# Two of four weight sums made by adding DMAs, and two groups of seven products in every gate-and-up block of FFN 2

## The chip, the cores and the metric

The kernel runs on one core of a Trainium2 chip. The metric is device time in microseconds (us), as the median of several runs. The engines are named as in the profile: PE (TensorE, matmuls), PEld (its weight loads), DVE (VectorE), ACT (ScalarE), POOL (GpSimd) and SP (SyncE, which issues most DMAs). L512 is line 512 of the kernel.

## What is computed

One layer of an encoder for 256 rows of width 2048, in float32. The parts that matter here are its two feed-forward halves:

```
x += 0.5 * (silu(h @ w_gate) * (h @ w_up)) @ w_down      h = RMSNorm(x)
```

with `w_gate` and `w_up` of 2048 x 5632 and `w_down` of 5632 x 2048. FFN 1 comes first, FFN 2 after the mixing part (an SSM and a stick-breaking attention, joined by `w_out`); a gated embedding ends the layer.

## The kernel before, in words

All weights are read once, in raw tiles of 512 x 512 (1 MB, `raw`, five buffers). To keep float32 precision, each half of a raw tile (128 x 1024) is split into two float32r parts: ACT casts it (`whi`, L181) and DVE subtracts the cast from it (`wlo`, L184). The activations are split likewise. A product is then three matmuls in place of one: high x high, low x high and high x low (L305, L306, L310 in `gemm_half`; L480, L481, L483 in `Seven.product`).

FFN gate and up run over blocks f = 0 to 10 of 512 columns. In a block, gate and up each need four quarters of the inner dimension (512 rows each, kb = 0 to 3), for two row tiles. There are two ways to do a quarter:

- `column` (L524): one side's quarter, two halves of a raw tile, 24 matmuls of 128x512 and 2 splits; gate and up together 48 matmuls and 4 splits.
- `chunk` (L490): gate and up of the quarter together in seven products (Strassen's scheme in Winograd's form), each 6 matmuls, 42 in all. The activation's four sums are made once (`sum_forms`). The weights' four sums are made for each group by DVE (`add`, L485 to L488): t1 = b11 + b12, t2 = t1 + b22, t4 = t2 + b21, t3 = b12 + b22, where b11 and b21 are the halves of gate's raw tile, b12 and b22 those of up's. Each of the seven operands is split; the sums' parts are called `shi` and `slo` (three buffers each), those of plain weights `whi` and `wlo` (four each). The sums lie in a tag `sum` of two buffers.

A block thus takes 186 matmuls with one group and 180 with two. FFN 2's blocks 1 to 10 alternate: odd blocks have two groups (`two`, L590), even blocks one. FFN 1 has plain blocks to f = 6, one group in 7 and 9 and two in 8 and 10. The down projections use groups as well, three in each FFN, by a written plan (L673 to L676).

The banks of the seven products are read when their last group is done: `opened` (L575) and `gated` (L580) by copies and adds of ACT and DVE, then L606 and L608, and two block transposes (L216).

The recorded program is put in order by a scheduler: each engine's instructions stand in one fixed order, and an engine that waits for one holds all behind it. `step()` lets helpers put their small work between the products. POOL issues few DMAs: x is written to a scratch tensor (L1453) and fetched again for each FFN's down projection (L150).

Of the kernel before, what the change touches and what calls it, by code (L numbers as in the profile page):

```python
# [13 lines left out]
ALU = mybir.AluOpType  # L14
# [19 lines left out]
def layer_kernel(ctx: ExitStack, tc: tile.TileContext, a: dict, shapes: dict, out: bass.AP):  # L34
    nc = tc.nc
# [27 lines left out]
    def uid(s):  # L63
        count[0] += 1
        return f"{s}_{count[0]}"
# [4 lines left out]
    def com(tag):  # L70
        return get(comp, tag, *{"sg": (1024, 1), "h": (1024, 2), "sq": (NB, 1), "mid": (2048, 1)}[tag])

    def phase(name):
        return tc.tile_pool(name=name, bufs=1, reuse_waits="tile")
# [24 lines left out]
    def step():  # L99
        for g in list(beside):  # L100
            if next(g, beside) is beside:
                beside.remove(g)

    def finish(g):
        for _ in g:
            pass
# [315 lines left out]
    def whole_rows(pool, parts):  # L422

        hi, lo = parts
        u = pool.tile([P, 2, NB], F32, tag="sum", name=uid("whole"), bufs=2)
        nc.vector.tensor_tensor(
            out=u.rearrange("p j n -> p (j n)"), in0=hi.bitcast(F32).rearrange("p j t -> p (j t)"),
            in1=lo.bitcast(F32).rearrange("p j t -> p (j t)"), op=ALU.add,
        )
        return u.rearrange("p j n -> p (j n)").rearrange("p (j x b) -> p j x b", j=4, b=32)  # L430

    def sum_forms(pool, u, kind="n"):

        sums = pool.tile([P, 2, NB], F32, tag="sum", name=uid("rows"), bufs=2)
        s = sums.rearrange("p j n -> p (j n)").rearrange("p (z j x b) -> p z j x b", z=4, j=2, b=32)
        (a11, a21), (a12, a22) = ([u[:, k : k + 2, 4 * t : 4 * t + 4] for t in range(TT)] for k in (0, 2))
        for z, (x, y, op) in enumerate((
            (a21, a22, ALU.subtract), (s[:, 0], a11, ALU.subtract),
            (a11, a21, ALU.subtract), (a12, s[:, 1], ALU.add),
        )):  # L440
            nc.vector.tensor_tensor(out=s[:, z], in0=x, in1=y, op=op)
        both = halves(kind)
        split(*both, sums.rearrange("p j n -> p (j n)").rearrange("p (z t) -> p z t", z=4))
        return both

    class Seven:
# [43 lines left out]
        def chunk(self, kb, final=()):  # L490

            raws = []
            for w, n0 in self.ws:
                raw = wp.tile([P, 4, NB], F32, tag="raw", name=uid("raw"), bufs=5)
                nc.sync.dma_start(
                    raw, w[4 * kb * P : 4 * (kb + 1) * P, n0 : n0 + NB].rearrange("(j p) n -> p j n", p=P)
                )
                raws.append(raw)
            b11, b21, b12, b22 = (raw[:, 2 * h : 2 * h + 2, :] for raw in raws for h in range(2))
            parts, sums = self.act(kb), self.sums(kb)  # L500

            def whole(k, t):
                return [[u[:, 2 * k + j, t * P : (t + 1) * P] for j in range(2)] for u in parts]

            def summed(z):
                return [[u[:, z, j * P : (j + 1) * P] for j in range(2)] for u in sums]

            self.product(1, whole(0, 0), b11, False, final)
            t1 = self.add(b11, b12)
            self.product(5, summed(0), t1, True, final)  # L510
            step()
            t2 = self.add(t1, b22)  # L512
            self.product(6, summed(1), t2, True, final)
            t4 = self.add(t2, b21)
            self.product(4, whole(1, 1), t4, True, final)
            step()
            t3 = self.add(b12, b22)
            self.product(7, summed(2), t3, True, final)
            self.product(2, whole(1, 0), b21, False, final)
            step()  # L520
            self.product(3, summed(3), b22, False, final)
            step()

        def column(self, side, kbs, final=False):  # L524
# [14 lines left out]
    def ffn(i, xn, nxt, bg=None):  # L539
# [23 lines left out]
        for f in range(NF):  # L563
            if prep and f == early:
                finish(prep)
                side.close()
                prep = None
                sevens = pools.enter_context(phase(f"sums{i}"))
                hp = pools.enter_context(phase(f"h{i}b"))
                sums = [sum_forms(sevens, whole_rows(sevens, xn(kb)), "h") for kb in range(2)]  # L570
            if sevens and f:
                sg, hh = com("sg"), com("h")
                gate_cols, up_cols = ([u[:, t * NB : (t + 1) * NB] for t in range(TT)] for u in (sg, hh))

                def opened(s, g=gate_cols, u=up_cols):  # L575
                    nc.scalar.copy(g[0], s.bank(1))
                    nc.vector.tensor_tensor(out=u[0], in0=s.bank(6), in1=g[0], op=ALU.add)
                    nc.vector.tensor_tensor(out=u[1], in0=s.bank(7), in1=u[0], op=ALU.add)

                def gated(s, g=gate_cols, u=up_cols, hh=hh):  # L580
                    for z, (ps, other) in enumerate(((s.bank(2), g[0]), (s.bank(4), u[1]))):
                        nc.vector.tensor_tensor(out=g[z], in0=ps, in1=other, op=ALU.add)
                        nc.scalar.activation(g[z], g[z], AF.Silu, scale=xn.rs(z))
                    v = hh.rearrange("p (t n) -> p t n", t=TT)
                    nc.vector.tensor_tensor(
                        out=v, in0=s.bank(5).unsqueeze(1).to_broadcast([P, TT, NB]), in1=v, op=ALU.subtract
                    )

                s = Seven(xn, lambda kb: sums[kb], ((wg, f * NB), (wu, f * NB)), sevens)
                two = f % 2 == (0 if bg else 1)  # L590
                if f == early:
                    s.column(0, (1, 2, 3))
                    s.chunk(0, (*shared, 2, 4))
                    put_off(0, opened, s)
                elif two:
                    s.chunk(0)
                    s.column(0, (2, 3))
                    s.chunk(1, (*shared, 2, 4))
                    put_off(0, opened, s)
                else:  # L600
                    s.chunk(0, shared)
                    put_off(0, opened, s)
                    s.column(0, (1, 2, 3), True)
                put_off(0, gated, s)
                s.column(1, (2, 3) if two and f != early else (1, 2, 3), True)
                nc.vector.tensor_tensor(out=hh, in0=s.banks[3.8], in1=hh, op=ALU.add)  # L606
                for t in range(TT):
                    nc.vector.scalar_tensor_tensor(  # L608
                        out=up_cols[t], in0=up_cols[t], scalar=xn.rs(t), in1=gate_cols[t], op0=ALU.mult, op1=ALU.mult
                    )  # L610
                put_off(2, turned, hp, f, hh)
                continue

            def gate():
                for t in range(TT):
                    nc.scalar.activation(sg[:, t * NB : (t + 1) * NB], pg[t], AF.Silu, scale=xn.rs(t))

            first = ()
            if f == 0 and bg:
                warm_up(10)  # L620
                first = first_quarters(wg, xn)
            if f == 0 and not bg:
                both = gemm_pair(xn, ((wg, 0), (wu, 0)), KD)
                pg = next(both)
                sums = [sum_forms(sevens, whole_rows(sevens, xn(kb))) for kb in range(2)]
            else:
                pg = gemm_block(xn, wg, f * NB, KD, first)
            sg = com("sg")
            if f == 0 and bg:
                for n in range(ND):  # L630
                    put_off(n, load_x, n)
                    put_off(n + 2, xn.squares, n)
                put_off(6, gate)
            else:
                gate()
            pu = gemm_block(xn, wu, f * NB, KD) if f or bg else next(both)
            if prep and f == 0:
                start(prep)
            hh = com("h")
            for t in range(TT):  # L640
                nc.vector.scalar_tensor_tensor(
                    out=hh[:, t * NB : (t + 1) * NB], in0=pu[t], scalar=xn.rs(t),
                    in1=sg[:, t * NB : (t + 1) * NB], op0=ALU.mult, op1=ALU.mult,
                )
            put_off(2, turned, hp, f, hh)
# [31 lines left out]
        for n in range(0, ND, 2):  # L677
# [17 lines left out]
            for u in plan:  # L695
                kb, final = int(u[1:]), u == plan[-1]
# [759 lines left out]
    mix.close()  # L1456

    ffn(2, n2, npl)


# [201 lines left out]
```

## Time and profile before

| what | value |
|---|---|
| median of 3 runs | 1852.45 us (1851.65 to 1853.28) |
| the profiled execution | 1852.7 us |
| its span | 1850.6 us, clock granted in full |
| ACT busy | 1027.4 us, 56% |
| POOL busy | 63.3 us, 3% |
| read from HBM | 373.46 MB, 208 GB/s with what is written over the span |

The engines work side by side, so their busy times do not add up. An idle engine costs time only where the engine that bounds the kernel waits for it. In the rows of groups, the number behind the second bar is the idle time of the engine just before these instructions, and behind the arrow is what ended it. In the rows of windows each engine has its busy time and its count of instructions; the last two columns are the mean busy share of the 16 DMA engines and the rate.

### The profile page before, as it was taken

What the parts mean: (1) busy time and instruction counts of PE and PEld (TensorE: products, weight loads), DVE (VectorE), ACT (ScalarE), POOL (GpSimd) and SP (SyncE); (2) the same over time, 40 slices, a digit from 0 to 9 for tenths busy, and PEclk for the clock granted to TensorE, in tenths of its full rate; (3) what the DMA queues carried; (4) which work ended last, traced back from release to release, by engine and by line L of the source; (5) the groups of instructions that cost most, each with busy time, mean ns of one, the idle gap of its engine ahead of it and who ended that gap; (6) DMA issues with size and microseconds to landing.
All of it is one profiled execution on the core that took longest, in us unless ns stands there. A gap on an engine that the chain in (4) does not pass through costs nothing.

```text
span 1850.6 us, 23946 instructions
## 1 busy us (share of the span) xinstructions
PE 1838.3 (99%) x9032; PEld 1518.5 (82%) x9032; DVE 1460.6 (79%) x1718; ACT 1027.4 (56%) x1187; POOL 63.3 (3%) x108
## 2 busy tenths in 40 slices
PE   9999999999999999999999999999999999999998
PEld 7888888778888888888897888888888888888887
DVE  8967665998888876687567798989898978887665
ACT  7444443655564656365685565655555555565654
POOL 0011000000000000010021000000000000000000
PEclk9999999999999999999999999999999999999999
DMA  9888868566756567675646776665656675666663
GB/s 334 281 274 277 252 217 246 173 228 200 241 196 213 192 217 248 190 262 166 216 142 218 224 262 216 235 206 198 218 198 219 207 244 185 223 195 217 208 219 125
DMA packets 232307, 406.36 MB, mean 220 GB/s; under 512 B 26784, under 2 KB 50720, under 8 KB 231904
## 3 DMA queue, kind: packets, MB, share of 16 engines
q1 hardware_dynamic: 227824, 392.81, 63.8%
q0 software_dynamic: 3648, 10.62, 1.8%
q8 instruction: 70, 1.15, 0.2%
q10 hardware_dynamic: 720, 1.41, 0.2%
q14 instruction: 45, 0.37, 0.1%
HBM read 373.46 MB, written 11.93 MB: 208 GB/s over the span
## 4 chain that ended last, share of the span: by engine, by line
PE 92%; DVE 3%; DMA 2%; ACT 2%; SPq 1%; issue 1%; DVEq 0%; ACTq 0%
PE acc L305 18%; PE acc L310 18%; PE acc L306 18%; PE aux L305 7%; PE aux L306 7%; PE aux L310 7%; PE acc L480 3%; PE acc L481 2%; PE acc L483 2%; PE aux L480 2%; PE aux L483 2%; PE aux L481 2%; DVE wlo L184 1%; SPq L1170 1%; DMA raw<-in_w_in 1%
## 5 line engine op out<-in xcount | busy, mean ns | idle before, releaser
L181 ACT CAST whi<-raw 128x1024 fp32r<-128x1024 f32 x639 | 668.1, 1052 | 684.8 <-PE acc L306 388.9
L184 DVE TENSOR_TENSOR wlo<-raw,whi 128x1024 fp32r<-128x1024 f32 x639 | 772.0, 1221 | 297.9 <-ACT whi L181 295.1
L305 PE MATMUL acc<-whi,nhi 128*128 128x512 f32 x1232 | 482.9, 392 | 1.8 <-ACT whi L181 1.7
L306 PE MATMUL acc<-whi,nlo 128*128 128x512 f32 x1232 | 479.9, 390 | 0.0
L310 PE MATMUL acc<-wlo,nhi 128*128 128x512 f32 x1232 | 340.6, 389 | 0.2 <-DVE wlo L184 0.2
L305 PEld LDWEIGHTS acc<-whi,nhi 128*128 128x128 f32 x1232 | 231.5, 188 | 52.2 <-ACT whi L181 3.0
L310 PEld LDWEIGHTS acc<-wlo,nhi 128*128 128x128 f32 x1232 | 231.2, 188 | 48.8 <-DVE wlo L184 0.6
L306 PEld LDWEIGHTS acc<-whi,nlo 128*128 128x128 f32 x1232 | 231.6, 188 | 47.2
L306 PE MATMUL acc<-whi,hlo 128*128 128x512 f32 x376 | 146.4, 389 | 0.0
L305 PE MATMUL acc<-whi,hhi 128*128 128x512 f32 x376 | 146.3, 389 | 0.0
L181 ACT CAST shi<-sum 128x1024 fp32r<-128x1024 f32 x108 | 113.4, 1052 | 43.1 <-DVE sum L487 39.6
L306 PE MATMUL aux<-whi,hlo 128*128 128x512 f32 x344 | 133.8, 389 | 0.0
L305 PE MATMUL aux<-whi,hhi 128*128 128x512 f32 x344 | 133.8, 389 | 0.0
L184 DVE TENSOR_TENSOR slo<-sum,shi 128x1024 fp32r<-128x1024 f32 x108 | 130.9, 1216 | 0.6 <-ACT shi L181 0.5
L310 PE MATMUL acc<-wlo,hhi 128*128 128x512 f32 x376 | 114.6, 389 | 0.2 <-DVE wlo L184 0.2
L310 PE MATMUL aux<-wlo,hhi 128*128 128x512 f32 x344 | 106.0, 389 | 0.0
L306 PE MATMUL aux<-whi,nlo 128*128 128x512 f32 x240 | 93.4, 389 | 0.0
L305 PE MATMUL aux<-whi,nhi 128*128 128x512 f32 x240 | 93.4, 389 | 0.0
L306 PEld LDWEIGHTS acc<-whi,hlo 128*128 128x128 f32 x376 | 70.6, 188 | 15.1 <-DVE hlo L184 0.4
L310 PEld LDWEIGHTS acc<-wlo,hhi 128*128 128x128 f32 x376 | 70.5, 188 | 15.2 <-DVE wlo L184 0.6
L305 PEld LDWEIGHTS acc<-whi,hhi 128*128 128x128 f32 x376 | 70.6, 188 | 14.6
L306 PEld LDWEIGHTS aux<-whi,hlo 128*128 128x128 f32 x344 | 64.6, 188 | 13.5
(345 smaller groups left out, 2162.6 us busy)
## 6 DMA issues: line engine op xcount, KB each, us to landing
raw<-in_ffn_w_up SPq DMA_DIRECT2D x88, 1024.0 KB, 5.8
raw<-in_ffn_w_down SPq DMA_DIRECT2D x88, 1024.0 KB, 5.1
raw<-in_ffn_w_gate SPq DMA_DIRECT2D x86, 1024.0 KB, 6.2
raw<-in_w_in SPq DMA_DIRECT2D x32, 1024.0 KB, 5.7
raw<-in_w_out SPq DMA_DIRECT2D x16, 1024.0 KB, 5.3
raw<-in_w_ple_gate SPq DMA_DIRECT2D x16, 1024.0 KB, 5.1
hT<-mid SPq DMA_DIRECT2D x160, 64.0 KB, 3.5
h<-mid SPq DMA_DIRECT2D x176, 32.0 KB, 3.6
```

Of the source, the lines that this page charges most:

```text
L181: copy = nc.scalar.copy(hi, src)
L184: nc.vector.tensor_tensor(out=lo, in0=src, in1=hi.bitcast(F32), op=ALU.subtract)
L305: nc.tensor.matmul(ps[t], lhsT=lh, rhs=hi[:, j, cols], start=start and j == 0, stop=False)
L306: nc.tensor.matmul(ps[t], lhsT=ll, rhs=hi[:, j, cols], start=False, stop=False)
L310: nc.tensor.matmul(ps[t], lhsT=lh, rhs=lo[:, j, cols], start=False, stop=stop and j == 1)
L480: nc.tensor.matmul(ps, lhsT=lh[j], rhs=hi[:, j], start=begin and j == 0, stop=False)
L481: nc.tensor.matmul(ps, lhsT=ll[j], rhs=hi[:, j], start=False, stop=False)
L483: nc.tensor.matmul(ps, lhsT=lh[j], rhs=lo[:, j], start=False, stop=z in final and j == 1)
L1170: nc.sync.dma_start(zt[0][p1 : p1 + HC, z], sv[p0 : p0 + HC, r % 2 * 2 + r // 2])
```

## The change

In `chunk`, t3 and t4 are no longer DVE's. Two DMAs issued by POOL add in place: b22 is added onto b12 in the raw tile, after t1 has read b12, and b21 is added onto t2, after product 6 has been split from it. Products 7 and 4 take their operands from there. The order of the products as written becomes 6, 5, 1, 2, 3, 7, 4. All groups are changed, in both FFNs and in the downs (27 groups before). Beside that, every block of FFN 2 from 1 to 10 has two groups (32 groups in all).

```
-            self.product(1, whole(0, 0), b11, False, final)
             t1 = self.add(b11, b12)
+            nc.gpsimd.dma_start(b12, b22, accum_op=ALU.add)
+            t2 = self.add(t1, b22)
+            self.product(6, summed(1), t2, True, final)
+            nc.gpsimd.dma_start(t2, b21, accum_op=ALU.add)
             self.product(5, summed(0), t1, True, final)
             step()
-            t2 = self.add(t1, b22)
-            self.product(6, summed(1), t2, True, final)
-            t4 = self.add(t2, b21)
-            self.product(4, whole(1, 1), t4, True, final)
-            step()
-            t3 = self.add(b12, b22)
-            self.product(7, summed(2), t3, True, final)
+            self.product(1, whole(0, 0), b11, False, final)
             self.product(2, whole(1, 0), b21, False, final)
             step()
             self.product(3, summed(3), b22, False, final)
+            self.product(7, summed(2), b12, True, final)
+            step()
+            self.product(4, whole(1, 1), t2, True, final)
             step()
...
-                two = f % 2 == (0 if bg else 1)
+                two = f % 2 == 0 if bg else True
```

In the changed kernel the adding DMAs are lines 509 and 512. Both versions of `chunk` are equally long, so all lines outside it keep their numbers.

## The prediction

> **What bounds the kernel now.** I read the page's first lines and its engine and DMA rows, then the windows of the stage that the change rebuilds, then the waits there, the chain of waits, and the DMA issues.
>
> ```profile
> span 1850.6 us, 23946 instructions
> PE 1838.3 (99%) x9032; PEld 1518.5 (82%) x9032; DVE 1460.6 (79%) x1718; ACT 1027.4 (56%) x1187; POOL 63.3 (3%) x108
> ...
> q1 hardware_dynamic: 227824, 392.81, 63.8%
> q0 software_dynamic: 3648, 10.62, 1.8%
> ```
>
> TensorE (PE) is busy for all but 12.3 us of the span. To be faster, the kernel needs fewer matmuls or must lose some of those 12.3 us; work taken off VectorE (DVE) buys nothing by itself.
>
> The stage that gains groups of seven is FFN 2's gate and up, from about 1090 to 1510 us. I cut it at the gate's Silu of every second block, so that each window holds a block with one group and a block with two.
>
> ```profile
> core 0: us, PE busy (x) PEld busy (x) DVE busy (x) ACT busy (x) POOL busy (x), PEclk, DMA share, GB/s
> 1120.80:1204.10 83.30, 83.30 (x368) 68.67 (x367) 75.23 (x74) 45.95 (x48) 0.00 (x0) 1.00 0.66 215
> 1204.10:1287.90 83.80, 83.80 (x370) 69.10 (x369) 75.62 (x74) 45.80 (x49) 0.00 (x0) 1.00 0.65 213
> 1287.90:1371.90 84.00, 84.00 (x371) 69.26 (x370) 75.32 (x74) 45.67 (x49) 0.00 (x0) 1.00 0.64 213
> 1371.90:1455.30 83.40, 83.40 (x368) 68.58 (x367) 75.51 (x74) 45.65 (x48) 0.00 (x0) 1.00 0.64 215
> ```
>
> Four times the same picture: PE is never idle, at full clock; DVE is busy 75.4 of 83.6 us, the DMA engines 65%. DVE's spare 8.2 us a pair is not free to take at any moment, but the waits say what it is:
>
> ```profile
> engine line waited for: us in total, times, longest us
> ...
> ACT whi L181 <- PE acc L306: 62.8, 40, 1.9
> ACT whi L181 <- PE acc L481: 39.6, 22, 4.5
> ACT whi L181 <- PE aux L306: 37.6, 28, 1.7
> DVE wlo L184 <- ACT whi L181: 37.3, 35, 1.8
> ```
>
> The casts (ACT) wait for PE to give back a buffer, and DVE waits for the casts. So the operands are ready before PE wants them, and a short stall of DVE is made up from that lead.
>
> **The change part by part.** *Matmuls removed.* A group takes one quarter of the inner dimension (512 rows, gate and up) in 7 products of 6 matmuls, 42 in place of 48. FFN 2's blocks 2, 4, 6, 8 and 10 get a second group: 5 x 6 = 30 matmuls fewer. Their price, from the chain of waits in a stage where PE never waits:
>
> ```profile
> 99.06 0.91 PE acc L310 x4
> ...
> 101.78 0.91 PE acc L310 x4
> ...
> 104.50 0.91 PE acc L310 x4
> ```
>
> Twelve matmuls (4 of L310, 4 each of L305 and L306 between) in 2.72 us are 0.2267 us each. The check: a pair of blocks has 186 + 180 = 366 matmuls, 83.0 us by this price, against 83.3 to 84.0 in the windows. So 30 x 0.2267 = **6.8 us less**, if PE stays the bound; a pair becomes 2 x 180 x 0.2267 = 81.6 us.
>
> *DVE work.* Each group has now two adds (L487) instead of four; t3 and t4 go to two DMAs.
>
> ```profile
> L184 DVE TENSOR_TENSOR wlo<-raw,whi 128x1024 fp32r<-128x1024 f32 x29 | 34.8, 1215 | 7.8 <-ACT whi L181 7.8
> L184 DVE TENSOR_TENSOR slo<-sum,shi 128x1024 fp32r<-128x1024 f32 x12 | 14.6, 1216 | 0.0
> L487 DVE TENSOR_TENSOR sum<-sum,raw 128x1024 f32<-128x1024 f32 x6 | 7.3, 1220 | 0.0
> L487 DVE TENSOR_TENSOR sum<-raw,raw 128x1024 f32<-128x1024 f32 x3 | 3.6, 1216 | 0.0
> L487 DVE TENSOR_TENSOR sum<-raw 128x1024 f32<-128x1024 f32 x3 | 3.6, 1214 | 0.0
> ```
>
> These are DVE's large instructions of the first window: 41 subtractions and 12 adds, 53 per pair. Afterwards a pair has 2 x (14 + 8) = 44 subtractions and 8 adds, 52. One instruction less at 1.22 us: 75.4 becomes 74.2 us, in a pair of 81.6. DVE's spare time is 7.4 us where it was 8.2. The DMAs thus pay for the second group almost exactly, and nothing is over. ACT gains 3 casts of 1.05 us a pair and stays under 50 of 81.6.
>
> *The adding DMAs.* There are 32 groups (27 before), so 64 DMAs of 512 KB, issued by POOL, nothing like which is in the trace. Their price has two sides. **Throughput:** q1 moved 392.81 MB in 63.8% of 1850.6 us, 3.0 us per MB of all 16 engines, so a plain copy of 0.524 MB takes 1.6. An add in place fetches two operands where a copy fetches one. Bounds: one pass (1.6) and three, two fetched and one written as if in turn (4.8). I take two, 3.2: the fetching is what doubles. Eight a pair then add 25.6 us to 0.65 x 83.6 = 54.3, 79.9 of 81.6 us, 98% by mean occupancy. That sounds full, but the engines can move faster than their mean:
>
> ```profile
> DMA  6999971832222259999999999999999994891002
> GB/s 116 300 397 321 385 265 57 321 105 53 53 53 52 63 95 283 406 238 347 395 387 410 388 385 392 392 382 383 390 392 382 385 349 123 313 395 48 13 0 20
> ```
>
> These rows cover 1040 to 1090 us: when asked, the engines kept 385 to 390 GB/s. By that a pair's 17.9 MB of loads take 46 us and the eight adds 21.5 (1.05 MB each), 83% together. So the throughput suffices at two passes, tightly, and not at three.
>
> [...]
>
> **Landing time** L, from the end of t1 to the semaphore:
>
> ```profile
> scr_m<-m POOLq DMA_DIRECT2D x4, 512.0 KB, 4.9
> ...
> scr_x<-x POOLq DMA_DIRECT2D x8, 256.0 KB, 2.7
> ...
> zt<-mid SPq DMA_DIRECT2D x32, 32.0 KB, 2.0
> ```
>
> 32 KB land in 2.0 us, nearly all fixed. From 32 to 256 KB of a POOL DMA costs 0.7, so a pass of 512 KB 1.4: two passes land in 2.0 + 2.8 = 4.8 us. By the row of 512 KB, written early while the weights pressed hardest, a pass costs 2.9 and two land in 7.8. FFN 2's load lies between; I take 6. POOL itself has nothing else here but eight fetches of x in each FFN, of which the first stands before the last group's second add.
>
> *What waits behind an add.* In the changed program's order DVE does, for the second group of a block: t1, t2, the subtractions of products 1, 6, 5, 2, then product 7's, which needs `b12 += b22`, then 3's and a column's, then product 4's, which needs `t2 += b21`. ACT's casts stand in the same order, so a late DMA stops ACT first, with every later cast behind it, then DVE, then PE once its lead is used. How long DVE takes for five of them:
>
> ```profile
> 1164.38 1.22 DVE L184 TENSOR_TENSOR slo<-sum,shi 128x1024 fp32r<-128x1024 f32 x1
> ...
> 1168.92 1.22 DVE L184 TENSOR_TENSOR slo<-sum,shi 128x1024 fp32r<-128x1024 f32 x1
> ```
>
> Four steps in 4.54 us, 1.135 each. Product 7's turn comes 5 x 1.135 = 5.7 us after t1; its cast takes 1.05; the first add may land 4.6 us after t1 without loss. The second starts after product 6's subtraction and has again five steps, 4.6 us, plus whatever the first one held up, so it adds nothing. A group loses L - 4.6. Of a pair's four groups three stand like this; the fourth, at the head of a block, has a dozen instructions of the block before it in between and loses nothing until far higher. At L = 6 the loss is 3 x 1.4 = 4.2 us a pair, under the 7.4 spare. PE wants product 7 only after 6, 5, 1, 2 and 3 (6.8 us), so a stall of that size is not seen at once either. **Cost: nothing visible**, so long as 74.2 + 3 (L - 4.6) stays under 81.6, that is L under 7.1.
>
> *FFN 1 and the downs.* The groups there (6 and 3 + 3) also lose two adds each. That matters only where PE waits now, in FFN 1's blocks 7 to 9:
>
> ```profile
> 337.80 0.50 PE L480 MATMUL aux<-shi,hhi 128*128 128x512 f32 x1 [0.89 <-ACT shi L181]
> 366.04 0.50 PE L480 MATMUL acc<-shi,nhi 128*128 128x512 f32 x1 [0.97 <-ACT shi L181]
> 409.56 0.50 PE L480 MATMUL acc<-shi,nhi 128*128 128x512 f32 x1 [1.67 <-ACT shi L181]
> ```
>
> 3.5 us, all of it PE waiting for the cast of a sum, while DVE is behind. Two adds fewer are 2.4 us per group, but product 6, which needs both remaining adds, is now PE's first. I take 1.5 us off, between 3.5 off and 2 on. The downs have a single fill of sums per 40 us or more and PE without a gap; I cost them at nothing, up to 1 us if a raw buffer comes free late (two of the three left there are held until the second add has landed).
>
> **Sum.** The profiled execution took 1852.7 us, 2.1 outside the span; the median of the three runs is 0.25 lower. 1852.7 - 6.8 - 1.5 = 1844.4, on the median's scale **1844.2 us**. Its own range is 1841 (all of FFN 1's waits gone, a little of the rest) to 1848.
>
> **The rivals.**
> *The adds land late (slower).* The same sum with L = 8.5, a little above the heavy bound: 74.2 + 3 x 3.9 = 85.9 us a pair against 83.6 before, 5 pairs, +11.5: **1864**, FFN 1 unchanged. It decides from L = 7.7 (74.2 + 9.3 = 83.5, no gain left). For it: DVE has 0.8 us less slack a pair than before; the heavy row. Against: the weights take 65% here, not the 80 to 98% of the span's first slices.
> *Gain and stall cancel.* L between 7.4 and 8: **1851**.
> *The DMA engines become the bound.* At three passes a pair needs 54.3 + 38.4 = 92.7 us, +9.1 x 5 = +45: **1898**. Against: 385 GB/s and more where asked. It decides from an add of about 3.7 us.
> *The descriptors wait for DVE.* POOL writes them while DVE runs; if each add has to wait for one or two DVE instructions of 1.22 us, L = 6 becomes 8.4, a pair 85.6, **1863**. Against it:
>
> ```profile
> L150 POOL DMA_DIRECT2D x<-in_x x8 | 4.4, 551 | 182.8 <-DMA hT<-mid 179.8 <-DVE wlo L184 2.6 <-issue 0.2
> ```
>
> POOL's issues take 0.55 us beside a DVE that is busy most of the time. [...]
>
> **How the numbers follow.** Forecast 0.58; late landing 0.18; cancelled 0.12; DMA-bound 0.07; descriptors 0.05. The range 1841 to 1864 takes in the forecast, the cancelled case and most of the late and descriptor cases, about 0.85; above it lies the DMA-bound case. 0.2% is 3.7 us, about what a measurement of this kernel can tell from no change: faster is under 1848.7 and holds the forecast and a little of the cancelled case, 0.60; within, 0.13; slower, 0.27.
>
> **What would show it.** Right: 9002 matmuls; pairs of FFN 2 blocks of about 81.7 us with PE busy throughout; L509 and L512 landing in 5 to 7 us; ACT's waits for them under 2 us each; the DMA share there 0.8 to 0.95. Wrong: PE waiting for shi in FFN 2, adds landing in 8 us or more, casts waiting for raw (loads crowded out), or DVE busy as long as before in a longer pair.

## The result, and the profile after

The changed kernel takes **1880.48 us** (median of 5 runs, 1879.22 to 1883.90), the kernel before 1852.05 in the same session: a ratio of 1.0155, 95% interval 1.0144 to 1.0166. It is 28 us slower, where 8 us faster was forecast; it lies above the range too.

The first lines of the page and the two DMA queues, after:

```profile
span 1877.4 us, 24140 instructions
PE 1846.1 (98%) x9002; PEld 1514.4 (81%) x9002; DVE 1430.0 (76%) x1689; ACT 1032.4 (55%) x1202; POOL 118.7 (6%) x172
...
q1 hardware_dynamic: 227824, 392.81, 62.6%
q0 software_dynamic: 12864, 44.18, 11.4%
```

The 30 matmuls are gone (9032 to 9002) and DVE has 31 us less to do, and yet PE stands still for 31 us in place of 12. Where the time went is read by cutting the span at two places that both kernels have, FFN 2's first Silu (L616) and the last L606 of its gate and up:

| us of the profiled execution | before | after |
|---|---|---|
| up to FFN 2's first Silu (FFN 1's groups are in it) | 1086.4 | 1089.2 |
| FFN 2's gate and up | 420.5 | 444.1 |
| the rest, FFN 2's down | 343.7 | 344.1 |
| span | 1850.6 | 1877.4 |

So 23.6 of 26.8 us are lost in the stage that the prediction cut into pairs of blocks, 2.8 ahead of FFN 2, and nothing to speak of in the down. The same windows of pairs as in the prediction, after:

```profile
1129.90:1217.80 87.90, 85.44 (x367) 69.47 (x366) 74.43 (x73) 47.17 (x52) 7.02 (x8) 0.98 0.86 252
1217.80:1307.10 89.30, 84.35 (x357) 67.40 (x356) 74.46 (x73) 47.04 (x52) 7.03 (x8) 0.98 0.85 247
1307.10:1396.90 89.80, 85.76 (x366) 69.12 (x365) 74.29 (x73) 46.87 (x51) 7.03 (x8) 0.98 0.84 246
1396.90:1486.40 89.50, 84.86 (x366) 67.94 (x365) 74.64 (x73) 46.88 (x51) 7.02 (x8) 1.00 0.85 248
```

The first number behind the window is its length: 87.9 to 89.8 us where 81.6 was forecast. DVE's work is 74.4 us as worked out (74.2), the DMA share 0.85. PE, ACT, DVE and the DMA engines all have time over. That is the picture of a chain of waits, so the next view is that of the waits, from 1090 to 1510 us (the stage itself ends at 1533):

```profile
engine line waited for: us in total, times, longest us
...
ACT shi L181 <- DMA raw<-raw: 44.7, 18, 4.2
...
DVE slo L184 <- ACT shi L181: 40.9, 13, 6.2
...
ACT shi L181 <- DMA sum<-raw: 19.8, 4, 6.7
DVE sum L487 <- DMA raw<-in_ffn_w_up: 13.8, 7, 2.2
DVE wlo L184 <- ACT whi L181: 11.6, 7, 2.2
PE aux L480 <- DVE h L606: 10.5, 4, 3.0
```

Three kinds of waits are new. ACT waits for the first add (raw<-raw) in nearly every group and for the second (sum<-raw) four times, three of them over 6 us, and DVE waits behind ACT. DVE's t1 waits for a load of up. PE waits for L606. The main wait that DVE had before, for casts that PE held back, has shrunk from 37.3 to 11.6 us: the operands are no longer ready ahead of PE. DVE is always either busy or waiting, so its waits always fill a pair; whom it waits for is what tells. Before it was PE, by way of ACT; now it is the adds and the loads.

The timeline of the second pair shows these waits one by one (start, length, and in brackets the idle time before):

```profile
1242.71 1.23 DVE L184 TENSOR_TENSOR slo<-raw,shi 128x1024 fp32r<-128x1024 f32 x1 [1.31 <-ACT shi L181]
...
1252.01 1.22 DVE L184 TENSOR_TENSOR slo<-sum,shi 128x1024 fp32r<-128x1024 f32 x1 [5.80 <-ACT shi L181]
...
1258.39 1.23 DVE L487 TENSOR_TENSOR sum<-raw,raw 128x1024 f32<-128x1024 f32 x1 [1.03 <-DMA raw<-in_ffn_w_up]
...
1270.20 1.23 DVE L184 TENSOR_TENSOR wlo<-raw,whi 128x1024 fp32r<-128x1024 f32 x1 [1.98 <-ACT whi L181]
...
1291.40 1.23 DVE L184 TENSOR_TENSOR slo<-raw,shi 128x1024 fp32r<-128x1024 f32 x1 [2.52 <-ACT shi L181]
...
1298.11 1.23 DVE L487 TENSOR_TENSOR sum<-raw,raw 128x1024 f32<-128x1024 f32 x1 [2.07 <-DMA raw<-in_ffn_w_up]
```

14.7 us together, and 74.5 + 14.7 = 89.2 of the pair's 89.3. Product 7's operand costs 1.31, 1.98 (ACT stands at that cast for 2.19 us just before) and 2.52; product 4's 5.80; the up loads 3.1. The longest wait belongs to a second add. Its cast on ACT, and its issue on POOL:

```profile
1250.93 1.04 ACT L181 CAST shi<-sum 128x1024 fp32r<-128x1024 f32 x1 [6.35 <-DMA sum<-raw]
```

```profile
1239.53 0.88 POOL L512 DMA_DIRECT2D sum<-raw  x1 [2.48 <-DVE slo L184]
```

From issue to landing 11.3 us. At the same place in the third and fourth pair it is 11.7 and 11.2. In the first pair it is 6.7 and ACT does not wait for it; that pair is hardly shorter (87.9 us), for DVE waits 7.2 us by first adds there and 4.4 for loads. The DMA view of 1236 to 1253 us says what stood beside the add of the second pair:

```profile
DMA  2466899999396667558899999999999999998899
GB/s 63 104 142 109 157 195 193 193 284 193 60 195 159 188 217 198 169 135 207 260 267 263 296 260 248 243 265 287 231 219 270 282 333 282 258 222 282 255 272 299
...
sum<-raw POOLq DMA_DIRECT2D x1, 512.0 KB, 11.3
hT<-mid SPq DMA_DIRECT2D x7, 64.0 KB, 9.7
```

In every second block the turned h (hT<-mid, 16 small DMAs) goes out in the middle of the block, and two weight tiles follow it. Here the engines are full at 200 to 300 GB/s for the most part. Over all of the span the adds look as they were forecast:

```profile
raw<-in_ffn_w_gate SPq DMA_DIRECT2D x86, 1024.0 KB, 7.7
...
raw<-raw POOLq DMA_DIRECT2D x32, 512.0 KB, 5.8
sum<-raw POOLq DMA_DIRECT2D x32, 512.0 KB, 6.4
```

In FFN 2 (1090 to 1510 us) they take longer:

```profile
raw<-raw POOLq DMA_DIRECT2D x19, 512.0 KB, 6.3
sum<-raw POOLq DMA_DIRECT2D x19, 512.0 KB, 6.8
```

These times run from the issue, but the prediction counted L from the end of t1, 0.6 us earlier. Where ACT stands waiting, the start of product 7's cast gives that L. It is 5.8 to 6.3 us in nine of FFN 2's groups and 7.0 to 8.8 in ten; ACT was ready 4.2 us after t1 in most of them and 6.4 after it at every second block's head. A late one, whose t1 ended at 1192.54:

```profile
1200.94 1.05 ACT L181 CAST shi<-raw 128x1024 fp32r<-128x1024 f32 x1 [4.15 <-DMA raw<-raw]
```

### The profile page after: what moved, and what is told of

Read it like the earlier page. It is cut to its first block, busy times and chain, and to the rows that moved or that the text cites. A ratio compares the mean times of both kernels' runs of the same rounds, so it can differ in the third digit from the quotient of the medians.

```text
span 1877.4 us, 24140 instructions
## 1 busy us (share of the span) xinstructions
PE 1846.1 (98%) x9002; PEld 1514.4 (81%) x9002; DVE 1430.0 (76%) x1689; ACT 1032.4 (55%) x1202; POOL 118.7 (6%) x172
## 3 DMA queue, kind: packets, MB, share of 16 engines
q0 software_dynamic: 12864, 44.18, 11.4%
## 4 chain that ended last, share of the span: by engine, by line
PE 79%; DVE 9%; DMA 8%; issue 3%; ACT 1%; POOL 0%; DVEq 0%; SPq 0%; POOLq 0%; ACTq 0%
PE acc L305 17%; PE acc L310 17%; PE acc L306 17%; PE aux L310 5%; PE aux L305 5%; PE aux L306 5%; DMA sum<-raw 4%; DVE wlo L184 4%; DMA raw<-in_ffn_w_up 2%; PE acc L483 2%; DVE slo L184 2%; PE acc L480 2%; PE acc L481 2%; PE aux L480 1%; PE aux L481 1%
## 5 line engine op out<-in xcount | busy, mean ns | idle before, releaser
L181 ACT CAST shi<-sum 128x1024 fp32r<-128x1024 f32 x96 | 98.2, 1049 | 83.3 <-DVE sum L487 40.5
L184 DVE TENSOR_TENSOR slo<-sum,shi 128x1024 fp32r<-128x1024 f32 x96 | 114.8, 1218 | 34.5 <-ACT shi L181 34.5
L305 PE MATMUL acc<-whi,hhi 128*128 128x512 f32 x336 | 131.1, 390 | 0.3 <-ACT whi L181 0.3
L306 PE MATMUL acc<-whi,hlo 128*128 128x512 f32 x336 | 131.0, 390 | 0.0
L305 PE MATMUL aux<-whi,hhi 128*128 128x512 f32 x304 | 118.3, 389 | 0.0
L306 PE MATMUL aux<-whi,hlo 128*128 128x512 f32 x304 | 118.3, 389 | 0.0
L310 PE MATMUL acc<-wlo,hhi 128*128 128x512 f32 x336 | 102.6, 390 | 0.5 <-DVE wlo L184 0.3
L310 PE MATMUL aux<-wlo,hhi 128*128 128x512 f32 x304 | 93.8, 390 | 0.2
L509 POOL DMA_DIRECT2D raw<-raw x32 | 28.2, 880 | 773.4 <-DVE sum L487 266.8
L310 PE MATMUL aux<-wlo,nhi 128*128 128x512 f32 x240 | 74.0, 390 | 0.3 <-DVE wlo L184 0.3
```

Source lines behind the costliest of these rows:

```text
L181: copy = nc.scalar.copy(hi, src)
L184: nc.vector.tensor_tensor(out=lo, in0=src, in1=hi.bitcast(F32), op=ALU.subtract)
L305: nc.tensor.matmul(ps[t], lhsT=lh, rhs=hi[:, j, cols], start=start and j == 0, stop=False)
L306: nc.tensor.matmul(ps[t], lhsT=ll, rhs=hi[:, j, cols], start=False, stop=False)
L310: nc.tensor.matmul(ps[t], lhsT=lh, rhs=lo[:, j, cols], start=False, stop=stop and j == 1)
L509: nc.gpsimd.dma_start(b12, b22, accum_op=ALU.add)
```

## The experiments

The theory to test: **the adds land later than the order reads them, and their waits, with those for the buffers they hold, exceed DVE's spare time**. Within it stand three places: the lead of each add (T1), gate's raw buffer, which the second add holds (T2), and L606 behind product 7 at the head of a block (T3). The rivals: the doubled groups alone cost it (T0), or the traffic of the adds does, wherever their readers stand. Times are medians; each ratio is against the kernel before, run on the same chip.

| kernel | us | ratio, 95% interval |
|---|---|---|
| changed kernel | 1880.48 | 1.0155 (1.0144 to 1.0166) |
| e1 adds by DMA, groups spread as before | 1858.76 | 1.0034 (1.0023 to 1.0046) |
| e2 doubled groups, sums by DVE | 1854.59 | 1.0011 (1.0002 to 1.0021) |
| e3 adds of 64 KB | 1845.60 | 0.9962 (0.9947 to 0.9977) |
| e14 adds of 256 KB | 1846.24 | 0.9967 (0.9956 to 0.9978) |
| e6 copies in place of adds | 1846.38 | 0.9964 (0.9951 to 0.9977) |
| e7 first add alone | 1849.26 | 0.9981 (0.9972 to 0.9990) |
| e8 second add alone | 1854.55 | 1.0009 (1.0000 to 1.0019) |
| e16 first add, second only in the first quarter | 1862.41 | 1.0054 (1.0037 to 1.0071) |
| e17 each sum half by DMA, half by DVE | 1856.03 | 1.0017 (1.0008 to 1.0026) |
| e4 gate's buffer freed | 1878.87 | 1.0141 (1.0126 to 1.0156) |
| e10 one step more lead | 1874.70 | 1.0118 (1.0103 to 1.0133) |
| e5 column moved ahead of product 7 | 1858.05 | 1.0028 (1.0018 to 1.0037) |
| e11 the same, order held | 1859.63 | 1.0041 (1.0027 to 1.0055) |
| e18 the same, adds of 64 KB | 1846.56 | 0.9969 (0.9957 to 0.9981) |
| e12 the same, first add alone | 1850.97 | 0.9990 (0.9981 to 1.0000) |
| e15 the same, gate's buffer freed | 1875.72 | 1.0124 (1.0109 to 1.0140) |
| e9 traffic without readers, first try | 1910.19 | 1.0311 (1.0295 to 1.0326) |
| e13 traffic without readers | 1851.92 | 1.0006 (0.9992 to 1.0020) |

### The two halves of the change

e1 keeps the adds and takes the second groups away; e2 keeps the second groups and takes the adds away (the kernel before with the second line below).

```diff
 e1, in the changed kernel
-                two = f % 2 == 0 if bg else True
+                two = f % 2 == (0 if bg else 1)
 e2, in the kernel before
-                two = f % 2 == (0 if bg else 1)
+                two = f % 2 == 0 if bg else True
```

> The adding DMAs and the new order, with the groups spread as before (one and two in turn in FFN 2's gate and up, 9032 matmuls). DVE's work per pair of FFN 2 blocks falls to 41 subtractions and 6 adds, about 67 of 83.6 us, so its spare time is 16 us. Theory 'the DMAs cost waits' (late landings, raw buffers held, a PE hole at block heads): the stalls remain for the three groups but are paid out of the 16 us; 1850 to 1856 us. Theory 'the groups alone cost it, the DMAs are innocent': this kernel has DVE idle by 8 us more a pair and no second group, so like before or a little less, 1846 to 1852. If holes of PE show here too, 1858 or more, the spare time of DVE is not what decides.

> The doubled groups alone: the kernel before, with two groups in every block of FFN 2's gate and up, all four sums by DVE in the old order (9002 matmuls). DVE's work per pair is 75.4 + 3 subtractions + 4 adds = 83.9 us by the rows of before, PE's 81.6. Theory 'the groups alone cost it': DVE too full, 1875 to 1885 as in the changed kernel. Theory 'the DMAs cost it': a pair at 84 to 85 us, 1852 to 1858.

e2: 1854.59 us. T0 falls: the groups alone cost 2 us, though DVE is full as worked out (from 1090 to 1510 us; DVE's 412.95 is the third number after the length):

```profile
1090.00:1510.00 420.00, 414.20 (x1808) 338.19 (x1807) 412.95 (x399) 242.29 (x250) 4.36 (x8) 1.00 0.65 215
```

e1: 1858.76, above what the first theory gave and in the range put down for holes of PE. Its profiled execution is the quickest of seven (span 1854.5), and PE has no wait in FFN 2's gate and up there; where the other 2.5 us of the median lie is not known. By the cuts used above the profiled one loses 2.7 us in FFN 1 and 0.8 in FFN 2's gate and up, whose pairs take 81.7 to 84.0 us:

```profile
1294.74:1378.34 83.60, 83.60 (x368) 68.78 (x367) 69.10 (x68) 45.31 (x48) 5.26 (x6) 1.00 0.85 252
```

With DVE busy 69 us, the waits for the adds are paid out of its spare time, at the same DMA share of 0.85, and PE stays full. They are also fewer: from 1090 to 1510 us ACT waits 21.9 us for adds, in the changed kernel 64.5. So the loss in FFN 2 needs both halves: the adds' waits and a DVE with little to spare. FFN 1, which e1 has as the changed kernel has it, loses about the same as there (2.7 and 2.8 us).

### How long the add takes

e3 and e14 let the adds move less; e6 copies in place of adding. All three leave out a part of the sums of products 7 and 4, so they price the waits and do not compute the layer.

```diff
 e3
-            nc.gpsimd.dma_start(b12, b22, accum_op=ALU.add)
+            nc.gpsimd.dma_start(b12[:, :1, :P], b22[:, :1, :P], accum_op=ALU.add)
 e14
+            nc.gpsimd.dma_start(b12[:, :1], b22[:, :1], accum_op=ALU.add)
 e6
+            nc.gpsimd.dma_start(b12, b22)
 (the second add, t2 and b21, in the same way)
```

> The changed kernel whose adding DMAs move an eighth of each tile (128 rows of 512 B, 64 KB), so that seven eighths of the sums of products 4 and 7 are left out; DVE, ACT, PE and the waits' structure are as in the changed kernel. Theory 'landing time and held buffers': the adds land in 2 to 3 us, the stalls go, a pair is 81.6 to 82.5 us, 1843 to 1850 in all. Theory 'the groups and the new order cost it whatever the DMAs take': 1875 to 1882.

> The changed kernel with adds of half of each tile (256 KB; half of the sums of products 4 and 7 left out), in the same order. By the landings of 64 KB (3.2 and 2.5 us) and 512 KB (5.8 and 6.4) the adds should land in about 4.3 us, 1.5 to 2 earlier. Theory 'lateness has a threshold' (loss only past the lead of 4.6 us and DVE's spare time): close to the small adds, 1846 to 1853. If the loss goes with the bytes: half way, 1860 to 1865.

> The changed kernel with plain copies of the same size in place of the adds (b12 and t2 get b22 and b21, so the operands of products 7 and 4 lack their first terms); order and waits are the same. What is measured is the price of adding: if an add is two passes and a copy one, a copy lands 1.4 to 2.9 us earlier (3.5 to 4.5 median against 5.8 and 6.4) and takes about 1.6 us of all 16 engines against 2.8; then the landing is under or at the 4.6 us of lead and the time falls to 1845 to 1855. If copies land as late as adds, the size of the transfer beside the loads decides, not the adding, and the time stays over 1870.

1845.60, 1846.24 and 1846.38 us: where the adds land early, the kernel is 6 to 7 us ahead of the one before, of the 8 forecast. The time up to FFN 2's first Silu is 1085.0 in e3, 1.4 less than before (1.5 was forecast), and a pair:

```profile
1204.53:1286.87 82.34, 82.34 (x362) 67.55 (x361) 74.71 (x73) 48.01 (x51) 7.03 (x8) 1.00 0.71 223
```

The adds' issues in e14 (256 KB) and in e6 (copies of 512 KB), with the median from issue to landing:

```profile
raw<-raw POOLq DMA_DIRECT2D x32, 256.0 KB, 4.2
sum<-raw POOLq DMA_DIRECT2D x32, 256.0 KB, 3.8
```

```profile
q0 software_dynamic: 12864, 44.18, 6.6%
...
raw<-raw POOLq DMA_DIRECT2D x32, 512.0 KB, 4.2
sum<-raw POOLq DMA_DIRECT2D x32, 512.0 KB, 3.9
```

A landing 1.6 to 2.6 us earlier takes away all 34 us, by half the bytes or by not adding. The loss does not go with the bytes: at 64 and 256 KB an add it is absent, at 512 KB it is there in full. e6 also gives the price of adding: the queue's share before was 1.8% of 1850.6 us (33 us), so 64 copies take 6.6% x 1844.6 - 33 = 88 us of all engines, 1.4 each, and 64 adds 11.4% x 1877.4 - 33 = 181, 2.8 each: **two passes** (2.04).

### Traffic or waits

e9 and e13 keep all bytes of the adds, but give them places that nobody reads: t1 and t2 themselves.

```diff
 e9 (both adds behind product 5, neither on b12 or b21)
+            nc.gpsimd.dma_start(t1, t2, accum_op=ALU.add)
+            nc.gpsimd.dma_start(t1, t2, accum_op=ALU.add)
 e13
             self.product(5, summed(0), t1, True, final)
+            nc.gpsimd.dma_start(t1, t1, accum_op=ALU.add)
             step()
+            self.product(4, whole(1, 1), t2, True, final)
+            nc.gpsimd.dma_start(t2, t2, accum_op=ALU.add)
             self.product(1, whole(0, 0), b11, False, final)
```

> The changed kernel's traffic without its waits: two adds of 512 KB in every group, but both of t2 onto t1 after t1's last reader, so that no product waits for them and no raw buffer is held by them (products 7 and 4 get b12 and t2 without their second terms). DVE, ACT and PE have the same work as in the changed kernel. Theory 'waits' (lateness against the order, held buffers): 1844 to 1849. Rival 'traffic' (adds slow the loads, DVE or PE by being there): 1860 or more.

> The traffic of the adds without waits, made again: in the first trial t1 waited for the adds that were put into its own buffer (74.6 us of DVE's waits in FFN 2), which was a new wait and not the traffic. Now each group adds t1 onto itself after product 5 and t2 onto itself after product 4, which comes third in the group, so that each buffer has over 10 us until it is written again; nobody reads the sums, and no raw buffer is held (products 7 and 4 lack their second terms). Same bytes as the changed kernel. Theory 'waits': 1844 to 1850. Rival 'traffic': the 13 us that a longer lead did not win back are the price of the adds' presence, 1856 to 1862.

e9 missed its question. The second add waits for the first there, and t1's buffer isn't free when the next group wants it. DVE's waits in FFN 2:

```profile
DVE sum L487 <- DMA sum<-sum: 74.6, 14, 9.6
```

1910.19 us: an add that nobody reads still costs what its buffer is worth. e13 mends that: 1851.92 us, between its two forecasts. In the pairs the traffic costs nothing; this one has the DMA engines at 0.93 and takes what e3's takes:

```profile
1210.85:1293.15 82.30, 82.30 (x361) 67.56 (x360) 74.31 (x73) 47.84 (x51) 7.02 (x8) 1.00 0.93 268
```

The 7 us over e3's span are 2.7 before FFN 2 and 4.8 ahead of the first and behind the last of its pairs. So traffic as such is some 6 of the 35 us by the medians, and none of that lies in the pairs, where the change lost most. (The adds do not stand at quite the same moments of a group as in the changed kernel.)

### One add or both

```diff
 e7 (first add alone)
-            nc.gpsimd.dma_start(t2, b21, accum_op=ALU.add)
+            t4 = self.add(t2, b21)
 e8 (second add alone; t3 just ahead of product 7)
-            nc.gpsimd.dma_start(b12, b22, accum_op=ALU.add)
+            t3 = self.add(b12, b22)
 e16
+            if kb == 0:
                 nc.gpsimd.dma_start(t2, b21, accum_op=ALU.add)
+            else:
+                t2 = self.add(t2, b21)
```

> Only the first adding DMA of each group (product 7's operand); product 4's sum is DVE's again (4 more adds of 1.22 us a pair: DVE 79.1 of 81.6 us). Theory 'landing': product 7's stall stays, with less spare time of DVE to pay it: 1865 to 1885. The traffic is halved, so by the traffic rival about half of the loss goes, 1858 to 1868.

> Only the second adding DMA of each group (product 4's operand); product 7's sum is DVE's again, made just ahead of its subtraction (DVE 79.1 of 81.6 us a pair). The second add has seven steps of DVE from its issue to its turn, about 8 us, so by the theory 'landing' (6.4 us) its stalls nearly vanish: 1847 to 1856. If the second add alone costs as much as the first alone, the place in the order doesn't matter, and the traffic rival gains: 1858 to 1868.

> The first add of each group by DMA as in the kernel that had it alone (1849.3), the second one by DMA only in groups of the first quarter (at the head of a block in FFN 2), by DVE in those of the second. DVE 76.7 of 81.6 us a pair, 4.9 us spare in place of 2.5; the groups in the middle of a block, where the second add stalled DVE, are spared. If DVE's spare time is what the first add alone lacks: 1846 to 1848.5. If the second add's hold of gate's buffer or its lateness costs as much as it gives: 1849 to 1858.

1849.26, 1854.55 and 1862.41 us. Against e3 the first add alone costs 3.7 us, the second alone 9, both 35; in the first two prices the other sum is DVE's work again. My expectation for e7 (1865 to 1885) missed. Its first add lands no earlier, 6.0 us median, and ACT still waits 38.2 us for it in FFN 2 (44.7 in the changed kernel), but DVE waits 20 us in all where it waited 66. DVE's waits in FFN 2, e7:

```profile
DVE wlo L184 <- ACT whi L181: 15.0, 9, 2.8
DVE slo L184 <- ACT shi L181: 5.3, 3, 2.4
```

Nothing for loads, since gate's buffer is given back by DVE's own add, and that add of 1.22 us stands ahead of product 7's subtraction, so DVE has it to do while the first add is under way. DVE is fuller (78.4 us), yet no pair of e7 shows an idle PE:

```profile
1209.15:1291.07 81.92, 81.92 (x360) 67.19 (x359) 78.43 (x77) 46.84 (x52) 3.47 (x4) 1.00 0.80 250
```

Alone, the second add lands in 4.6 us in FFN 2; behind a first add, in 6.8 (above). Even alone it makes ACT wait 18.4 us there. e8:

```profile
sum<-raw POOLq DMA_DIRECT2D x19, 512.0 KB, 4.6
```

e16, slower than either of its ranges, shows that the second add hurts in the groups at the head of a block too. There product 7 stands ahead of L606 again, and PE's waits in FFN 2 have

```profile
PE aux L480 <- DVE h L609: 5.6, 4, 2.2
```

(L609 is L606 here). What makes up the rest of e16's 13 us over e7 was not taken apart.

e17 shares each sum, so that nothing is left out:

```diff
+            nc.gpsimd.dma_start(b12[:, :1], b22[:, :1], accum_op=ALU.add)
+            nc.vector.tensor_tensor(out=b12[:, 1:], in0=b12[:, 1:], in1=b22[:, 1:], op=ALU.add)
 (t2 and b21 in the same way)
```

> The changed kernel with each of the two sums shared: the first half of the tile (256 KB) by the adding DMA, the second half by DVE (0.6 us each, 8 a pair). All sums are whole. DVE 74.2 + 8 x 0.6 = 79 of 81.6 us a pair; the adds land in about 4.2 and 3.8 us as the half adds did (1846.2), inside their lead. Theory 'lead and DVE's spare time': no stall by adds, but only 2.6 us of DVE to spare a pair, 1846 to 1850, at or ahead of the first add alone (1849.3). If the smaller adds still stall: 1852 to 1858.

1856.03 us, in the range for adds that still stall. Its pairs take 81.4 to 84.4 us and FFN 1 loses 3.5. The half adds are not late by their median, but by place: the one issued at 1151.90 us, with the turned h before it, takes 7.0 us and stops DVE for 2.26. The DMA view of 1140 to 1165 us, e17:

```profile
sum<-raw POOLq DMA_DIRECT2D x1, 256.0 KB, 7.0
```

e14 has such waits too (10.5 us of ACT's for its second adds over the span, the latest landing 8.4 us from its issue), with 7 us of spare DVE time a pair to pay them from; e17 has less than half of that.

### Lead, buffers, and the order at the head of a block

e4 frees gate's raw buffer, e10 gives a step of lead and takes product 7 behind product 3, e5 and e11 put a quarter of a column between products 3 and 7, e11 with the order held on ACT and DVE.

```diff
 e4
-            nc.gpsimd.dma_start(t2, b21, accum_op=ALU.add)
+            nc.gpsimd.dma_start(t2, t1, accum_op=ALU.add)
 e10 (latest: the last cast and the last subtraction; product 4 in the same way)
+            with tc.issue_after(latest[0]), tc.issue_after(latest[1]):
                 self.product(7, summed(2), b12, True, final)
 e5 (e11: with e10's lines)
             self.product(3, summed(3), b22, False, final)
+            if between:
+                self.column(*between)
             self.product(7, summed(2), b12, True, final)
...
-                    s.chunk(0)
-                    s.column(0, (2, 3))
-                    s.chunk(1, (*shared, 2, 4))
+                    s.chunk(0, (), (0, (2,)))
+                    s.column(0, (3,))
+                    s.chunk(1, (*shared, 2, 4), (1, (2,)))
```

> The changed kernel whose second adding DMA reads t1 in place of the gate's raw tile (product 4 then gets a wrong operand): as many bytes, the same order, but gate's raw tile is free after product 2's subtraction instead of after the second add's landing, so the next group's load goes out earlier. Theory 'held raw buffers' as the main cause: the waits of t1 for the up load (2.2 us each) and those of Silu behind it go, about 5 us a pair, 1855 to 1862. Theory 'landing' as the main cause: 1870 to 1881.

> The changed kernel with one step more of lead for each add and nothing else: product 7's cast and subtraction are queued behind product 3's, product 4's behind product 7's (in the middle of a block the scheduler had put 7 ahead of 3). Lead of the first add from 4.6 to about 5.7 us beside a median landing of 5.8. Theory 'lead': each of 10 to 15 stalls gets about 1.1 us shorter, 11 to 17 us less, 1863 to 1870. Rival 'held buffers or order at block heads decide': within 5 us of the changed kernel, 1875 to 1883.

> The changed kernel with more time between the adds and their readers, nothing else taken away: in blocks with two groups one quarter of a column (two subtractions, 12 matmuls) that stood behind a group is put between product 3 and product 7. Product 7's cast then comes some 7 to 9 us after t1 in place of about 5. Theory 'the adds land later than their turn' (5.8 and 6.4 us median beside a lead of 4.6): most stalls of FFN 2 go, pairs of blocks from 89 to 82-84 us, 1845 to 1855. Rival 'the adds slow everything else (loads, DVE, ACT) by the traffic they make, wherever their readers stand': 1868 to 1882.

> The kernel with a quarter of a column between products 3 and 7, now with the order held on ACT and DVE (in the run before it the scheduler moved product 7 ahead of that column again, so its lead in the middle of a block stayed near 5 us). Lead of both adds 8 us or more. Theory 'lead' alone: no stall for an add is left, 1845 to 1849. If held raw buffers are the other half: DVE's waits for the up load (16.7 us over FFN 2 there) stay or grow, 1852 to 1860.

e4: 1878.87 us. The buffer is not the main cause, though the wait that T2 named is gone. DVE's waits in FFN 2, e4 (after: 40.9 and 13.8):

```profile
DVE slo L184 <- ACT shi L181: 45.4, 14, 7.3
...
DVE sum L487 <- DMA raw<-in_ffn_w_up: 1.5, 2, 1.3
```

About half of that time is found in the next stall: DVE's waits for casts grew by 6.1 us, and only 1.6 us were won.

e10: 1874.70 us, 5.8 less than the changed kernel and short of the 11 to 17 expected. L606 now comes out in time: PE's waits for it are 2.1 us (10.5 after):

```profile
PE aux L483 <- DVE h L611: 2.1, 4, 0.9
```

PE's waits for operands grew, however, so that all of its waits there are 15.7 us beside 17.4.

e5 and e11: 1858.05 and 1859.63 us; with more lead 21 to 22 us of the 35 over e3 come back. In e5 the scheduler moved product 7 ahead of the column again in the middle of a block, so only the heads gained lead for the first add; ACT's waits for adds fell from 64.5 to 18.1 us all the same. In e11 the waits for the adds are nearly gone (40.9 to 7.3), what is left is casts that PE holds back, and loads:

```profile
DVE wlo L186 <- ACT whi L183: 32.5, 16, 2.9
DVE sum L490 <- DMA raw<-in_ffn_w_up: 12.3, 7, 7.4
DVE slo L186 <- ACT shi L183: 7.3, 6, 2.3
```

So T1 is shown, and with T3, which the same order undoes (in e11 PE has no wait for L606's line left), it is some 21 of the 35 us. How these divide between the heads and the middles of the blocks was not told apart: e11 has more lead in the middle than e5 and is no faster. Three runs went after the other 13: e18 is e11 with e3's small adds, e12 is e11 with the first add alone (as in e7), e15 is e11 with e4's line.

> The held long lead with adds of an eighth of the tile (64 KB; the rest of the sums of products 4 and 7 left out): what the moved order costs by itself, without late adds and without buffers held by them. If the 13 us that the long lead did not win back belong to the new order itself (raw buffers held to the later products, the later end of a block): 1855 to 1860. If they belong to the adds (buffers held until they land, loads crowded): 1845 to 1849.

> The same held order with only the first add by DMA (product 4's sum by DVE): DVE 79.1 of 81.6 us a pair, gate's raw buffer free early, product 7's lead 8 us or more, so that neither late landings nor held gate buffers are left. If lead and buffers are the whole loss: 1844.5 to 1847, ahead of the kernel with the first add alone (1849.3). If DVE's spare time of 2.5 us a pair is too little for whatever else it waits for: 1849 to 1853.

> The held long lead with the second add reading t1 in place of gate's raw tile, so that gate's raw buffer is free after product 2 (product 4 gets a wrong operand; same bytes). Theory 'the rest of the loss is the raw buffer that the second add holds': from 1859.6 to 1846 to 1851. If up's raw buffer, held until product 7, or the traffic is the rest: 1855 to 1860.

e18: 1846.56 us, so the moved order costs nothing and the 13 us too belong to the adds. e12: 1850.97, no better than e7: where the first add is alone, lead is no longer what lacks. e15: 1875.72, which answers nothing, since reading t1 moved the hold to t1's buffer. DVE's waits, e15:

```profile
DVE sum L490 <- DMA sum<-sum: 16.0, 3, 6.0
```

**Open:** in e11 gate's loads land in 9.8 us and up's in 6.6, in e18 in 6.9 and 5.7. Whether the loads are late because the second add gives gate's buffer back late, or because the adds crowd them, was not told apart.

## Why the prediction was wrong

- *Matmuls removed, 6.8 us*: right. 9002, and with short adds the kernel takes 1845.6 to 1846.4, beside the forecast 1844.2.
- *DVE's work, 74.2 us a pair*: right (74.4).
- *Two passes*: right, 2.8 us of all engines against 1.4 for a copy. That the fetching is what doubles was the author's estimate; the runs show the price alone. *The rate*: "the engines can move faster than their mean", 385 to 390 GB/s, holds where large loads run alone (366 to 390 in the kernel before, from 1235.2 to 1242 us). In the middle of every second block, with the small DMAs of h and two adds, they gave mostly 200 to 300. The mean share (0.85, forecast 0.83 to 0.98) hid these 10 us. In the pairs traffic that nobody waits for costs nothing (e13: 82.3 us at a DMA share of 0.93, e3's 82.3 at 0.71).
- *Landing, L = 6*: mis-sized. From the issue and over the span the medians are 5.8 and 6.4, but from the end of t1, as L is defined, the first adds of FFN 2 took 5.8 to 6.3 us in nine groups and 7.0 to 8.8 in ten. The lead was 4.2 us where 4.6 was worked out. The formula 74.2 + 3 (L - 4.6) puts one L in three groups, so it has no place for the late ones. (By the rows that it uses, where 224 KB more cost 0.7 us, two passes land in 5.2 us and not in 4.8; the 6 does not hang on it.)
- *"so it adds nothing"*, of the second add: this step failed, and gave the longest waits. Behind a first add it lands 2.2 us later than alone (6.8 and 4.6), 11.2 to 11.7 us in one place of three of the four pairs, and there DVE waited 5.7 to 6.2 us for it.
- *The raw buffers at nothing*: failed. The second add holds gate's tile, and t1 waited for up's load in 13.8 us of FFN 2. It is no sum of its own, though: with the tile freed (e4), half of the wait returned at the casts.
- *"The fourth, at the head of a block ... loses nothing until far higher"*: failed. ACT was ready 6.4 us after t1 at these heads, later than elsewhere, but the first add took 8.5 to 8.8. Product 7 stood ahead of L606 on DVE, so a late first add held back the bank that PE wanted: 10.5 us of PE's waits, and the clock (below). Undone together with a step of lead it is 5.8 us (e10).
- *Spare time, 7.4 us a pair, from which stalls are paid*: the mechanism is right (e1, e7, e14 keep PE full with waits inside it). The waits were 13.4 to 15.4 us, where 4.2 was worked out. In the pair shown they were 5.8 for the first adds, 5.8 for a second and 3.1 for loads.
- *FFN 1, -1.5*: right with small adds (-1.4); with whole ones +2.8. ACT waits for adds there too, up to 4.1 us, and 1.8 of the 2.8 are there at FFN 1's last L606; the rest behind it was not traced.
- *The rivals*: "the adds land late" named the mechanism and the side. Its L of 8.5 everywhere gave 1864; by its own formula 1880 would be an L of 9.6 in three groups, and no first add of FFN 2 took over 8.8. "DMA-bound" is excluded by e13, "the descriptors wait for DVE" by e3, whose 64 issues are as many and whose POOL is busy as long (119.2 us, 118.7 in the changed kernel).

e7, the first add alone, is the one version with all sums whole that beats the kernel before clear of the interval, by 0.19% (0.10 to 0.28%).

## What to carry to other kernels

A DMA that stands in for an instruction of a nearly full engine is priced at each place by its own landing, with what is in flight there, against the steps left until its reader; a median or a mean share says nothing of the one place that stalls the queue (here 11.3 us, where the median of FFN 2 was 6.8). Count the buffers that it holds, and what stands behind its reader on every engine. Where one such DMA fits, a second one may not: here one cost 4 or 9 us, both 35, and halving their bytes brought all of it back.

## What the runs showed of the hardware

- An add in place costs twice a copy in the time of the DMA engines (2.8 and 1.4 us per 512 KB) and lands 1.6 to 2.5 us later. POOL issues it in 0.88 us; its fetches of x took 0.55 in the kernel before.
- Behind three waits of PE for L606, of 2.46, 2.97 and 2.50 us, matmuls ran at about half the clock (0.53, 0.51 and 0.54 granted); behind a fourth, of 2.52 us, they did not (1.00). What tells the four apart was not tested. The first of them in PE's timeline of the changed kernel, and then its windows (length, PE busy, its matmuls; the clock stands third from the end):

```profile
1183.37 0.47 PE L480 MATMUL aux<-whi,nhi 128*128 128x512 f32 x1 [2.46 <-DVE h L606]
```

```profile
1184.60:1188.00 3.40, 3.40 (x10) 2.66 (x9) 3.40 (x6) 1.02 (x1) 0.00 (x0) 0.53 0.95 349
1188.00:1191.00 3.00, 3.00 (x14) 2.42 (x13) 3.00 (x4) 0.00 (x0) 0.00 (x0) 0.96 0.36 77
```

  By PE's timeline the matmuls start every 0.43 us in the first stretch, from 1184.85 to 1188.25, and every 0.23 behind it: eight start where fifteen fit (the row also counts those that reach in from ahead). Three such stretches of 3.4, 3.1 and 3.1 us, one in each of the first three pairs, cost some 5 us by this count, hidden in "PE busy"; in the kernel before the clock was 1.00 in all four pairs.
